# The second MLP matrix by seven products in every other block, and low parts built by adding transfers, in a four-layer encoder step

## The chip, the cores and the metric

The kernel runs on one core of one Trainium2 chip. The metric is the device time of one execution in microseconds (us); "before" is the median of three runs.

## The reference

Four layers, each a token mixer (differential attention, a gated recurrence, banded attention, and differential attention again) and then a squared-ReLU MLP, each on the root-mean-square norm of the residual stream and added back to it. The tokens are one prompt of 512 and eight streams of 16, so 640 columns. The part that the change touches is the MLP (D = 1024, D_FF = 4096):

```
def sq_relu_mlp(h, w1, w2):
    return jnp.square(jax.nn.relu(h @ w1)) @ w2
...
xp = xp + sq_relu_mlp(rms_norm(xp, norm_mlp_g[layer]), mlp_w1[layer], mlp_w2[layer])
```

Everything is float32.

## The kernel before

The residual x lies in SBUF as eight tiles of 128 features x 640 tokens; a matmul takes a 128x128 piece of a weight and one half (320 columns) of the tokens. Both operands are kept as a sum of a high part (rounded to the fast fp32r format) and a low part (the rest), and each fp32 product is three matmuls: low weight by high data, high by low, high by high. In names, `wh`/`wl` are the two parts of a weight unit (128 partitions x 1024 columns, 512 KB), `hh`/`hl` those of the squared activation.

**Weights.** `weight_plan` lists all units in the order of their use and the class `Weights` walks it. A unit's data comes from DRAM into one of three `raw` buffers (L173, L180, queue of SP). `parts` then makes `wh` by a copy on ACT (L202) and `wl` by a subtraction on DVE (L203); there are three buffers of each (`WB = 3`). A buffer is free again after the last matmul that reads it, so ACT's copy for the unit three further on waits for that matmul. ACT, DVE, POOL and SP each work through their instructions in program order.

**First matrix.** Hidden rows are taken in 8 blocks of 512 (`NBLK`), each in two halves. All but the first half-block ("A") are done by seven products of a 2x2 split (half the rows by half the tokens) in place of eight ("P", functions `pair` and `product`, matmuls at L974 to L976). A half-block has four units: two are plain or nearly so, and two hold sums of weight quarters, which DVE adds up into `wsum` (L233 to L238) before they are split in two parts.

**Second matrix.** Every block is done plainly ("M", function `rows`, matmuls in `t_mm` at L433 to L435): four units a block, each by 2 output tiles x 2 token halves x 12 matmuls, 192 a block; each group of 12 fills one PSUM bank (`ps_mm`, `ps_s`), which DVE adds to x (L1074). `mlp_order` sets the order: block c of the second matrix is woven between the products of block c + 1 of the first.

**Norms.** Before each mixer and MLP the squares of x are summed over the feature tiles; some of these sums are made by DMA transfers on POOL's queue that add what they bring to what lies in the target (L332, 28 in all, SBUF to SBUF, 320 KB each).

Of the kernel before, what the change touches and what calls it, by code (L numbers as in the profile page):

```python
# [15 lines left out]
P = 128  # L16
# [15 lines left out]
WB = 3  # L32
HB = 16
# [4 lines left out]
NBLK = FF // 512  # L38
ROWS = (0, 4, 1, 5, 2, 6, 3, 7)
# [5 lines left out]
def mlp_order(last):  # L45

    out, rows, late = [], [], None

    def m_rows(c, lo, hi):
        return [("M", c, i, r, h) for i in range(lo, hi) for r in range(2) for h in range(2)]

    for c in range(NBLK):
        for j in range(2):
            if c == j == 0:  # L60
                out += [("A", r, h, part) for part in range(2) for r in range(2) for h in range(2)]
                continue
            out.append(("P", c, j, 1))
            if late and not rows:
                out.append(late)
                late = None
            out += [("P", c, j, n) for n in (2, 5, 6, 3, 7)]
            rows = m_rows(c - 1, 2 * j, 2 * j + 2) if c else []
            if rows:
                out.append(rows[0])  # L70
                out.append(("P", c, j, 4))
                out += rows[1:]
            else:
                late = ("P", c, j, 4)
            if c == 1 and j == 0:
                assert late is None
    if not last:
        out += m_rows(NBLK - 1, 0, 4)
    return out


UNIT_OF = {1: 0, 2: 0, 5: 1, 6: 1, 3: 2, 7: 2, 4: 3}


def weight_plan():

    plan = []
    for layer, kind in enumerate(KINDS):
# [20 lines left out]
        for o in mlp_order(last):  # L109
            if o[0] == "A":  # L110
                continue
            if o[0] == "P":
                key = ("P", o[1], o[2], UNIT_OF[o[3]])
                if key not in seen:
                    plan.append(("w1", 16 * layer + 2 * o[1] + o[2], key[3]))
            else:
# [11 lines left out]
def hybrid_encoder_kernel(ctx: ExitStack, tc: tile.TileContext, I, O):  # L128
# [16 lines left out]
    class Weights:  # L145
# [3 lines left out]
        def __init__(self):  # L149
# [4 lines left out]
            for k, (name, _, n) in enumerate(self.plan):  # L154
                if name == "w1":
# [10 lines left out]
        def load(self):  # L166
# [5 lines left out]
            if name == "w1":  # L172
                sp.dma_start(t, I[name][i][:, 1024 * hs_[0]:1024 * hs_[0] + 1024])  # L173
                self.pair.setdefault(i, []).append(t)
            else:
                o, w = sum(n[:hs_[0]]), sum(n[h] for h in hs_)
                dst, src = t[:, :w], self.source(name, i, o, w)
                if len(src.shape) == 3:
                    dst = dst.rearrange("p (t c) -> p t c", t=src.shape[1])
                sp.dma_start(dst, src)  # L180
                for h in hs_:
                    self.raw[k, h] = (t, sum(n[:h]) - o, h == hs_[-1])
            self.loaded += 1

# [14 lines left out]
        def parts(self, u, src, w):  # L199
            hi = wpool.tile([P, 1024], F32R, tag="wh", name="wh", bufs=WB)  # L200
            lo = wpool.tile([P, 1024], F32R, tag="wl", name="wl", bufs=WB)
            act.activation(hi[:, :w], src, AF.Copy)  # L202
            dve.tensor_sub(lo[:, :w], src, hi[:, :w].bitcast(F32))  # L203
            self.tiles[u] = (hi, lo)
            self.nsplit += 1

        def split(self):
# [5 lines left out]
            if name == "w1":  # L213
                self.split_pair(u, i, h)
# [3 lines left out]
            self.parts(u, t[:, o:o + w], w)  # L218
# [3 lines left out]
        def split_pair(self, u, i, h):  # L222
            a, b = self.pair[i][:2]
            if h == 0:
                self.parts(u, a, 1024)
            elif h == 3:
                self.parts(u, b[:, 512:], 512)
                del self.pair[i]
                self.load()
            else:  # L230
                t = self.work.tile([P, 1024], F32, tag="wsum", name="wsum", bufs=2)
                if h == 1:
                    dve.tensor_add(t[:, :512], b[:, :512], b[:, 512:])  # L233
                    dve.tensor_add(t[:, 512:], t[:, :512], a[:, :512])
                    self.pair[i].append(t)
                else:
                    dve.tensor_add(t[:, :512], self.pair[i][2][:, 512:], a[:, 512:])
                    dve.tensor_add(t[:, 512:], b[:, :512], a[:, :512])  # L238
# [38 lines left out]
    alam = const.tile([P, 2, 2, 2, 64], F32, name="alam")  # L277
    sp.dma_start(alam, bass.AP(tensor=I["alam"].tensor, offset=I["alam"].offset, ap=[[0, P], [1, 512]]))
# [9 lines left out]
    class Normed:  # L288
# [19 lines left out]
        def square(self, d):  # L308
# [15 lines left out]
            if n < 2:  # L324
                t = self.work.tile([P, N], F32, tag="sacc", name="sacc", bufs=2)
# [3 lines left out]
            sq = self.work.tile([P, N], F32, tag="sq", name="sq", bufs=3)  # L329
# [5 lines left out]
            if n == KT8 - 1:  # L335
                dve.tensor_add(self.sums[0], self.sums[0], self.sums[1])
                self.acc = self.sums[0]

# [20 lines left out]
    class Forms(Normed):  # L359
# [7 lines left out]
        def __init__(self, work, g, home):  # L367
# [3 lines left out]
            self.b12 = [None] * 4  # L371

# [26 lines left out]
        def build(self, k):  # L399
            g, g2, ng2 = self.gain(k), self.gain(k + 4), self.gain(k + 4, True)  # L400
            b = self.home("fs")
            act.activation(hs(b, 0), hs(x[k], 1), AF.Copy, scale=g)
            b12 = hs(b, 0)
# [10 lines left out]
            d1, d2 = self.home("fs"), self.home("fs")  # L414
# [53 lines left out]
    def attention(layer, kind, xg, aw, op):  # L468
# [19 lines left out]
        if is_a:  # L488
# [8 lines left out]
            lam_init = 0.8 - 0.6 * math.exp(-0.3 * layer)  # L497
            lp = aw.tile([P, 2, 64], F32, name="lp")
            dve.tensor_mul(lp, alam[:, idx, :, 0], alam[:, idx, :, 1])
            ld = aw.tile([P, 2], F32, name="ld")  # L500
            dve.tensor_reduce(ld, lp, axis=AX.X, op=ALU.add)
            le = aw.tile([P, 2], F32, name="le")
            act.activation(le, ld, AF.Exp)
            nlam = aw.tile([P, 1], F32, name="nlam")
            dve.tensor_sub(nlam, le[:, 1:2], le[:, 0:1])
            dve.tensor_scalar_add(nlam, nlam, -lam_init)
            lcol = aw.tile([P, 1], F32, name="lcol")
            dve.scalar_tensor_tensor(lcol, halves[:, 1:2], nlam, halves[:, 0:1], op0=ALU.mult, op1=ALU.add)
# [469 lines left out]
    def mlp(nx, hw, after, built):  # L978
# [7 lines left out]
        H, L = {}, {}  # L986
        units, left, banks_, st = {}, {}, {}, {}
# [17 lines left out]
        def finish(c, j, r, v):  # L1005
            act.activation(v, v, AF.Square)
            hi, lo = home("hh", F32R), home("hl", F32R)
            act.activation(hi, v, AF.Copy)
            dve.tensor_sub(lo, v, hi.bitcast(F32))
            H[c, 2 * j + r], L[c, 2 * j + r] = hi, lo  # L1010

        def pair(c, j, n):
# [12 lines left out]
            if n == 1:  # L1025
                p["a1"] = copy(acc)
                p["v1"] = hw.tile([P, N], F32, tag="v", name="v", bufs=4)
                p["v2"] = hw.tile([P, N], F32, tag="v", name="v", bufs=4)
# [6 lines left out]
            elif n == 3:  # L1035
                dve.tensor_add(hs(p["v1"], 1), acc, p["a2"])
                dve.scalar_tensor_tensor(p["v1"], p["v1"], 0.0, nx.b, op0=ALU.max, op1=ALU.mult)
                finish(c, j, 0, p["v1"])
# [3 lines left out]
            else:  # L1042
                dve.scalar_tensor_tensor(hs(p["v2"], 0), acc, 0.0, hs(nx.b, 0), op0=ALU.min, op1=ALU.mult)
                finish(c, j, 1, p["v2"])
# [15 lines left out]
        def first_out():  # L1060
            for r in range(2):
                v = hw.tile([P, N], F32, tag="v", name="v", bufs=4)
                for h in range(2):
                    dve.scalar_tensor_tensor(hs(v, h), banks_.pop((r, h))[:, :HALF], 0.0, hs(nx.b, h), op0=ALU.max, op1=ALU.mult)
                finish(0, 0, r, v)

# [13 lines left out]
        for n, o in enumerate(order):  # L1080
# [10 lines left out]
            elif o[0] == "P":  # L1091
                pair(*o[1:])
            else:
# [223 lines left out]
    hw = cm.__enter__()  # L1317
    cur = Normed(hw, 0, first=True)
# [6 lines left out]
    cur.rstd(KINDS[0] == 1)  # L1325
    def mlp_pool():
# [176 lines left out]
```

## Time and profile before

| | |
|---|---|
| median of three runs | 3144.65 us (3141.0 to 3146.62) |
| profiled execution, own time | 3146.26 us |
| profiled execution, span of the trace | 3144.5 us |
| mean granted TensorE clock | 0.993 |
| TensorE busy | 98% of the span |

The span is what the profiler saw from the first to the last instruction; the own time is the same execution as the device timed it, 1.8 us longer. The median of the runs lies 1.6 us under that execution.

### The profile page before, as it was taken

To read this page: it belongs to the slowest core of one execution; us is meant where nothing else is said; L and a number is where in the kernel's file an instruction comes from. 1 tells how busy PE (TensorE), PEld (TensorE's weight loads), DVE (VectorE), ACT (ScalarE), POOL (GpSimd) and SP (SyncE) were. 2 spreads that over 40 slices of the span, in tenths; PEclk is the share of its full clock that TensorE was granted. 3 is DMA by queue.
4 is the path that set the end of the run, shared out by engine and by line. 5 is a ranking of instruction groups with operands and counts; after the bars stand their busy time and mean duration, and the time that the engine had idled before them with its cause. 6 is when DMAs were issued, how large, how long until landed. Compare 5 with 4: busy or idle time off the path is not lost. (4 is left out here: it accounts for less than half of the span.)

```text
span 3144.5 us, 61475 instructions
## 1 busy us (share of the span) xinstructions
PE 3091.7 (98%) x24354; PEld 2954.5 (94%) x24354; DVE 2158.4 (69%) x4653; ACT 1533.4 (49%) x3084; POOL 510.4 (16%) x676
## 2 busy tenths in 40 slices
PE   8999999999999999999999999999999999999998
PEld 7888799999999999999988889999998887999998
DVE  7777686666688766666566677666677776866665
ACT  4666653333476533334566654333346665533333
POOL 5444200000044100000222200000043432000001
PEclk9999999999999999999999999999999999999999
DMA  6877622222312322223566532222257776222222
GB/s 229 279 264 262 222 78 81 81 81 79 102 61 69 84 81 81 81 81 104 190 204 198 175 104 74 81 78 79 93 181 275 265 263 228 76 76 81 81 81 101
DMA packets 169679, 423.49 MB, mean 135 GB/s; under 512 B 19248, under 2 KB 49968, under 8 KB 169392
## 3 DMA queue, kind: packets, MB, share of 16 engines
q1 hardware_dynamic: 144336, 394.51, 36.8%
q0 software_dynamic: 4032, 9.18, 1.7%
q10 hardware_dynamic: 21024, 15.89, 1.6%
q8 instruction: 192, 3.15, 0.4%
q14 instruction: 95, 0.78, 0.1%
HBM read 379.24 MB, written 18.50 MB: 126 GB/s over the span
## 5 line engine op out<-in xcount | busy, mean ns | idle before, releaser
L202 ACT ACTIVATE wh<-raw 128x1024 fp32r<-128x1024 f32 (+1 forms) x396 | 381.8, 965 | 490.9 <-PE ps_t L975 220.3
L203 DVE TENSOR_TENSOR wl<-raw,wh 128x1024 fp32r<-128x1024 f32 (+1 forms) x396 | 451.0, 1139 | 165.0 <-ACT wh L202 162.2
L537 PE MATMUL ps_mm<-wh,xh 128*128 128x256 f32 x1344 | 388.9, 290 | 7.5 <-ACT wh L202 7.2
L539 PE MATMUL ps_mm<-wh,xl 128*128 128x256 f32 x1344 | 387.3, 288 | 6.1 <-DVE xl L303 6.1
L538 PE MATMUL ps_mm<-wl,xh 128*128 128x256 f32 x1344 | 386.4, 288 | 0.0
L435 PE MATMUL ps_s<-hh,wl 128*128 128x320 f32 x1024 | 316.5, 309 | 0.0
L433 PE MATMUL ps_s<-hh,wh 128*128 128x320 f32 x1024 | 316.4, 309 | 0.0
L433 PE MATMUL ps_mm<-hh,wh 128*128 128x320 f32 x1024 | 316.4, 309 | 0.0
L434 PE MATMUL ps_mm<-hl,wh 128*128 128x320 f32 x1024 | 316.4, 309 | 0.0
L435 PE MATMUL ps_mm<-hh,wl 128*128 128x320 f32 x1024 | 316.4, 309 | 0.0
L434 PE MATMUL ps_s<-hl,wh 128*128 128x320 f32 x1024 | 316.4, 309 | 0.0
L537 PEld LDWEIGHTS ps_mm<-wh,xh 128*128 128x128 f32 x1344 | 256.8, 191 | 24.2 <-issue 9.1
L539 PEld LDWEIGHTS ps_mm<-wh,xl 128*128 128x128 f32 x1344 | 256.5, 191 | 23.1 <-issue 14.8
L538 PEld LDWEIGHTS ps_mm<-wl,xh 128*128 128x128 f32 x1344 | 256.9, 191 | 9.0 <-issue 6.6
L202 ACT ACTIVATE wh<-wsum 128x1024 fp32r<-128x1024 f32 x120 | 126.4, 1053 | 254.4 <-PE ps_s L434 225.5
L332 POOL DMA_DIRECT2D sacc<-sq x28 | 24.9, 888 | 1322.9 <-ACT sq L330 1272.9
L435 PEld LDWEIGHTS ps_s<-hh,wl 128*128 128x128 f32 x1024 | 192.2, 188 | 0.1
L433 PEld LDWEIGHTS ps_s<-hh,wh 128*128 128x128 f32 x1024 | 192.2, 188 | 0.0
L435 PEld LDWEIGHTS ps_mm<-hh,wl 128*128 128x128 f32 x1024 | 192.2, 188 | 0.0
L434 PEld LDWEIGHTS ps_mm<-hl,wh 128*128 128x128 f32 x1024 | 192.2, 188 | 0.0
L434 PEld LDWEIGHTS ps_s<-hl,wh 128*128 128x128 f32 x1024 | 192.2, 188 | 0.0
L433 PEld LDWEIGHTS ps_mm<-hh,wh 128*128 128x128 f32 x1024 | 192.2, 188 | 0.0
(439 smaller groups left out, 8752.4 us busy)
## 6 DMA issues: line engine op xcount, KB each, us to landing
raw<-in_w SPq DMA_DIRECT2D x260, 512.0 KB, 3.5
kk<-in_cak SPq DMA_DIRECT2D x128, 512.0 KB, 6.9
vv<-in_cav SPq DMA_DIRECT2D x128, 512.0 KB, 5.7
raw<-in_wax SPq DMA_DIRECT2D x48, 512.0 KB, 5.1
kk<-in_cck SPq DMA_DIRECT2D x32, 512.0 KB, 4.5
vv<-in_ccv SPq DMA_DIRECT2D x32, 512.0 KB, 4.7
raw<-in_wcx SPq DMA_DIRECT2D x24, 512.0 KB, 4.6
sacc<-sq POOLq DMA_DIRECT2D x28, 320.0 KB, 5.0
```

Of the source, the lines that this page charges most:

```text
L202: act.activation(hi[:, :w], src, AF.Copy)
L203: dve.tensor_sub(lo[:, :w], src, hi[:, :w].bitcast(F32))
L332: pool.dma_start(self.sums[n % 2], sq, accum_op=ALU.add)
L433: pe.matmul(acc[:, :HALF], lhsT=wh[:, cs], rhs=a, start=k == 0, stop=False)
L434: pe.matmul(acc[:, :HALF], lhsT=wh[:, cs], rhs=b, start=False, stop=False)
L435: pe.matmul(acc[:, :HALF], lhsT=wl[:, cs], rhs=a, start=False, stop=k == ks - 1)
L537: pe.matmul(acc[:, :256], lhsT=xg.hi[k][:, ts], rhs=wh[:, cs], start=k == 0, stop=False)
L538: pe.matmul(acc[:, :256], lhsT=xg.hi[k][:, ts], rhs=wl[:, cs], start=False, stop=False)
L539: pe.matmul(acc[:, :256], lhsT=xg.lo[k][:, ts], rhs=wh[:, cs], start=False, stop=k == KT8 - 1)
```

## The change

1. **Seven products in the second matrix.** In the blocks of `SCHEME` (0, 2, 4, 6) of every layer the new function `second` ("Q") does the second matrix by seven products too. A half-block of 512 output features is 84 matmuls; six fill a bank before DVE adds it to x or subtracts it, and some banks are added to two or three targets, with more matmuls in between. `finish` builds the forms that this needs of the activation: sums and differences of quarters, then their high and low parts (`dh`, `dl`, 128x1280, and `hb`). The units come as for the first matrix, two of four as sums of quarters made by DVE.
2. **Low parts by adding transfers.** For the plain units (`w1a`, the units of the blocks 1, 3, 5 and 7 of `w2`, and the first unit of each pair, for both matrices) `parts` gets the unit's place in DRAM. ACT writes minus the high part into `wl` (the copy with scale -1 rounds to fp32r), POOL starts a transfer that brings the same 512 KB from DRAM again and adds them there, and then ACT makes `wh`. DVE's subtraction is gone for these units. There are 168 such transfers: 68 of one piece (`in_w1`, 128x1024) and 100 of two pieces (`in_w2`, 128x2x512).
3. **Pools.** `wl` has four buffers (`WL = 4`), `HB` is 14, the activation tile `v` is 128x1280 and in two buffers, a new tag `HD` holds `fs`, `dh` and `dl` in four, and the squares of the norms lie in other pools. The small numbers of the differential attention (`nlam`, `lcol`) are made once at the start.

In all: TensorE 384 matmuls fewer. DVE has 200 subtractions of 1024 columns fewer, and more: 64 of 1024, 32 of 1280, 160 of 512, 352 of 320; 32 of 640 are gone. ACT has 168 copies of 1024 more for the minus parts, POOL 168 transfers more, SP as many as before.

```diff
-HB = 16
+WL = 4
+HB = 14
 PAIR = (1024, 1024)
 K1 = 4
 RB = 3
 RT = 28
 NBLK = FF // 512
+SCHEME = (0, 2, 4, 6)
 ROWS = (0, 4, 1, 5, 2, 6, 3, 7)
 LEAD = 6
...
+    def second(c, j):
+        if c < 0:
+            return []
+        if c in SCHEME:
+            return [("Q", c, j, n) for n in (1, 2, 5, 6, 3, 7, 4)]
+        return [("M", c, i, r, h) for i in (2 * j, 2 * j + 1) for r in range(2) for h in range(2)]
 
     for c in range(NBLK):
...
+            if m:
+                out += late + m[1:-1]
+                late = m[-1:]
+    out += late
     if not last:
-        out += m_rows(NBLK - 1, 0, 4)
+        out += second(NBLK - 1, 0) + second(NBLK - 1, 1)
...
-        def parts(self, u, src, w):
+        def parts(self, u, src, w, dram=None):
+
             hi = wpool.tile([P, 1024], F32R, tag="wh", name="wh", bufs=WB)
-            lo = wpool.tile([P, 1024], F32R, tag="wl", name="wl", bufs=WB)
-            act.activation(hi[:, :w], src, AF.Copy)
-            dve.tensor_sub(lo[:, :w], src, hi[:, :w].bitcast(F32))
+            lo = wpool.tile([P, 1024], F32R, tag="wl", name="wl", bufs=WL)
+            if dram is not None:
+                act.activation(lo[:, :w], src, AF.Copy, scale=-1.0)
+                self.start(pool, lo[:, :w], dram, accum_op=ALU.add)
+                act.activation(hi[:, :w], src, AF.Copy)
+            else:
+                dst, low = hi[:, :w], lo[:, :w]
+                if len(src.shape) == 3:
+                    dst, low = (v.rearrange("p (t c) -> p t c", t=src.shape[1]) for v in (dst, low))
+                act.activation(dst, src, AF.Copy)
+                dve.tensor_sub(low, src, dst.bitcast(F32))
             self.tiles[u] = (hi, lo)
...
-            self.parts(u, t[:, o:o + w], w)
+            dram = self.source(name, i, sum(n[:h]), w) if name in ("w1a", "w2") else None
+            self.parts(u, t[:, o:o + w], w, dram)
             if last:
...
             if h == 0:
-                self.parts(u, a, 1024)
+                self.parts(u, a, 1024, self.rows(name, i, 0))
             elif h == 3:
...
+        def finish(c, j, r, v):
+
+            s = v[:, r * N:r * N + N]
+            act.activation(s, s, AF.Square)
+            if c in SCHEME and r == 0:
+                t = home("hb", F32R)
+                parts(hs(t, 0), hs(t, 1), hs(s, 0))
+                H[c, 2 * j], L[c, 2 * j] = hs(t, 0), hs(t, 1)
+                return
+            hi, lo = home("hh", F32R), home("hl", F32R)
+            parts(hi, lo, s)
             H[c, 2 * j + r], L[c, 2 * j + r] = hi, lo
+            if c in SCHEME:
+
+                b = [v[:, i * HALF:(i + 1) * HALF] for i in range(4)]
+                dve.tensor_sub(b[0], b[0], b[1])
+                dve.tensor_sub(b[1], b[3], b[1])
+                dve.scalar_tensor_tensor(b[3], b[0], -1.0, b[3], op0=ALU.mult, op1=ALU.subtract)
+                dve.scalar_tensor_tensor(b[2], b[3], -1.0, b[2], op0=ALU.mult, op1=ALU.subtract)
+                dh = hw.tile([P, 2 * N], F32R, tag="HD", name="dh", bufs=4)
+                dl = hw.tile([P, 2 * N], F32R, tag="HD", name="dl", bufs=4)
+                parts(dh, dl, v)
+                hb, lb = H[c, 2 * j], L[c, 2 * j]
+                fs = {1: (hb, lb), 2: (hs(hi, 0), hs(lo, 0)), 3: (hs(hi, 1), hs(lo, 1))}
+                for i, n in enumerate((5, 7, 4, 6)):
+                    fs[n] = tuple(t[:, i * HALF:(i + 1) * HALF] for t in (dh, dl))
+                F[c, j] = fs
...
+        def second(c, d, n):
+
+            key = ("Q", c, d, UNIT_OF[n])
+            w = unit(key, 1 if n == 4 else 2)
+            z = {1: 1, 6: 1, 7: 1, 4: 1, 2: 2, 5: 4, 3: 4}[n]
+            for i in range(2):
+                if n in (1, 2, 5):
+                    zs[z, i] = bank(ACC[z > 1])
+                acc = zs[z, i][:, :HALF]
+                for j in range(2):
+                    m = 2 * i + j
+                    o = (2 * m + n - 1) * P if n < 3 else (m + (4 if n in (6, 7) else 0)) * P
+                    cs = slice(o, o + P)
+                    a, b = F[c, j][n]
+                    st_ = n in (1, 2, 5) and j == 0
+                    pe.matmul(acc, lhsT=w[0][:, cs], rhs=a, start=st_, stop=False, skip_group_check=True)
+                    pe.matmul(acc, lhsT=w[0][:, cs], rhs=b, start=False, stop=False, skip_group_check=True)
+                    pe.matmul(acc, lhsT=w[1][:, cs], rhs=a, start=False, stop=j == 1, skip_group_check=True)
+                r = x[4 * d + 2 * i], x[4 * d + 2 * i + 1]
+                if n in (1, 2):
+                    dve.tensor_add(hs(r[0], 0), hs(r[0], 0), acc)
+                elif n in (6, 3):
+                    dve.tensor_add(hs(r[0], 1), hs(r[0], 1), acc)
+                elif n in (5, 7):
+                    dve.tensor_sub(hs(r[1], 1), hs(r[1], 1), acc)
+                else:
+                    dve.tensor_sub(hs(r[1], 0), hs(r[1], 0), acc)
+            used(key)
 
```

Three places show how the order of instructions moves (names with numbers are buffers in the order in which they are taken).

**ACT, split of the weights in the middle of an MLP.** Before, ACT makes one copy of a unit and goes on:

```order
L202 ACTIVATE wh_8843<-raw_8738 128x1024
L202 ACTIVATE wh_8877<-raw_8774 128x1024
L202 ACTIVATE wh_8932<-wsum_8929 128x1024
L1006 ACTIVATE v_8756<-v_8756 128x640
L1008 ACTIVATE hh_8883<-v_8756 128x640
```

Now, with `wsum` units ahead as there, a plain unit has two copies, the minus part `wl` first:

```order
L230 ACTIVATE wh_9711<-wsum_9708 128x1024
L1047 ACTIVATE hh_9692<-v_9599 128x640
L230 ACTIVATE wh_9748<-wsum_9745 128x1024
L223 ACTIVATE wl_9777<-raw_9673 128x1024
L225 ACTIVATE wh_9776<-raw_9673 128x1024
L1053 ACTIVATE v_9599<-v_9599 128x640
```

The unit 9776/9777 has its low part begun by ACT in row 4 and finished by POOL's transfer, one of these (all of POOL's instructions of this stretch):

```order
L195 DMA wl_9509<-in_w1 128x1024
L195 DMA wl_9637<-in_w2 128x2x512
L195 DMA wl_9777<-in_w1 128x1024
L195 DMA wl_9905<-in_w2 128x2x512
L195 DMA wl_9978<-in_w2 128x2x512
```

What moved: the low part of such a unit comes from ACT and a transfer and no longer from DVE. The copy `wh_9748` in front of it and the buffer of `wl_9777` both wait for the last matmul of the same earlier unit (9636/9637).

**TensorE, second matrix.** Before, a plain group takes both parts of its unit from its first three matmuls on:

```order
L433 MATMUL ps_mm_8936<-hh_8305,wh_8843 128x320
L434 MATMUL ps_mm_8936<-hl_8306,wh_8843 128x320
L435 MATMUL ps_mm_8936<-hh_8305,wl_8844 128x320
L433 MATMUL ps_mm_8936<-hh_8361,wh_8843 128x320
L434 MATMUL ps_mm_8936<-hl_8362,wh_8843 128x320
L435 MATMUL ps_mm_8936<-hh_8361,wl_8844 128x320
L433 MATMUL ps_mm_8936<-hh_8566,wh_8843 128x320
L434 MATMUL ps_mm_8936<-hl_8567,wh_8843 128x320
```

Now, in the block 0 of the first layer (`wh_9748` is a unit of the second matrix, `wh_9776` the first unit of the next half-block of the first):

```order
L1011 MATMUL ps_t_9852<-f1_6551,wh_9776 128x320
L1012 MATMUL ps_t_9852<-f1_6551,wh_9776 128x320
L1011 MATMUL ps_t_9891<-fbh_6593,wh_9776 128x320
L1012 MATMUL ps_t_9891<-fbl_6594,wh_9776 128x320
L1149 MATMUL ps_mm_9717<-dh_8951,wh_9748 128x320
L1150 MATMUL ps_mm_9717<-dl_8952,wh_9748 128x320
L1151 MATMUL ps_mm_9717<-dh_8951,wl_9749 128x320
L1149 MATMUL ps_mm_9717<-dh_9221,wh_9748 128x320
L1150 MATMUL ps_mm_9717<-dl_9222,wh_9748 128x320
L1151 MATMUL ps_mm_9717<-dh_9221,wl_9749 128x320
L1013 MATMUL ps_t_9852<-f1_6551,wl_9777 128x320
L1011 MATMUL ps_t_9852<-f1_6626,wh_9776 128x320
```

What moved: the matmuls with `wl_9777` stand behind those with `wh_9776` and behind other work; from the last matmul that reads unit 9636/9637 to the first one that reads `wl_9777` there are 47 matmuls.

**TensorE, a bank used again.** Also now, the bank `ps_mm_9725`, first the last matmul of a group and then the next group's first:

```order
L1151 MATMUL ps_mm_9725<-dh_9221,wl_9749 128x320
L1011 MATMUL ps_t_9891<-fbh_6850,wh_9776 128x320
L1012 MATMUL ps_t_9891<-fbl_6851,wh_9776 128x320
L1013 MATMUL ps_t_9891<-fbh_6850,wl_9777 128x320
L1149 MATMUL ps_mm_9717<-dh_8951,wh_9811 128x320
L1150 MATMUL ps_mm_9717<-dl_8952,wh_9811 128x320
L1151 MATMUL ps_mm_9717<-dh_8951,wl_9812 128x320
L1149 MATMUL ps_mm_9717<-dh_9221,wh_9811 128x320
L1150 MATMUL ps_mm_9717<-dl_9222,wh_9811 128x320
L1151 MATMUL ps_mm_9717<-dh_9221,wl_9812 128x320
L1149 MATMUL ps_mm_9725<-dh_8951,wh_9811 128x320
```

Between the two, DVE has to add the bank's first half to x; nine matmuls lie between.

## Rows read from the trace of the kernel before

**Rows 1.** The page, part 1: busy time of the engines.

```profile
PE 3091.7 (98%) x24354; PEld 2954.5 (94%) x24354; DVE 2158.4 (69%) x4653; ACT 1533.4 (49%) x3084; POOL 510.4 (16%) x676
```

**Rows 2.** Inside MLPs: stretch, PE, PEld, DVE, ACT, POOL busy, PEclk, DMA share, GB/s.

```profile
436.00:840.00 404.00, 404.00 (x2759) 404.00 (x2758) 265.86 (x406) 158.23 (x214) 4.37 (x4) 1.00 0.25 83
...
sum 1164.00, PE 1164.00 PEld 1164.00 DVE 758.88 ACT 445.67 POOL 7.89; mean PE 388.00 PEld 388.00 DVE 252.96 ACT 148.56 POOL 2.63
```

**Rows 3.** Timeline of PE inside an MLP: start us, duration us, instruction.

```profile
679.78 0.31 PE L433 MATMUL ps_mm<-hh,wh 128*128 128x320 f32 x1
...
681.54 0.31 PE L433 MATMUL ps_s<-hh,wh 128*128 128x320 f32 x1
```

**Rows 4.** Timeline of DVE there (idle before, releaser, in brackets).

```profile
680.38 1.22 DVE L203 TENSOR_TENSOR wl<-raw,wh 128x1024 fp32r<-128x1024 f32 x1
681.52 1.22 DVE L203 TENSOR_TENSOR wl<-wsum,wh 128x1024 fp32r<-128x1024 f32 x1
682.65 0.48 DVE L1074 TENSOR_TENSOR x<-x,ps_mm 128x320 f32<-128x320 f32 x1
683.05 0.82 DVE L1009 TENSOR_TENSOR hl<-v,hh 128x640 fp32r<-128x640 f32 x1
```

**Rows 5.** Timeline of PE and ACT: a buffer's last readers, and its next copy.

```profile
693.57 0.31 PE L975 MATMUL ps_o<-fel,wh 128*128 128x320 f32 x1
...
693.91 0.63 ACT L202 ACTIVATE wh<-raw 128x512 fp32r<-128x512 f32 x1 [1.18 <-PE ps_o L975]
```

**Rows 6.** Timeline of ACT inside an MLP.

```profile
679.10 1.06 ACT L202 ACTIVATE wh<-raw 128x1024 fp32r<-128x1024 f32 x1 [4.59 <-PE ps_t L975]
680.06 1.04 ACT L202 ACTIVATE wh<-wsum 128x1024 fp32r<-128x1024 f32 x1
```

**Rows 7.** Timeline of ACT and POOL: a square and its adding transfer.

```profile
412.17 0.72 ACT L330 ACTIVATE sq<-x 128x640 f32<-128x640 f32 x1
...
413.19 0.87 POOL L332 DMA_DIRECT2D sacc<-sq  x1 [3.04 <-ACT sq L330]
```

**Rows 8.** Tile sacc: its adding transfers, issue (ns) and landing (us).

```profile
L332 POOL DMA_DIRECT2D sacc<-sq x28: 854/870/1072, 405.3 to 2699.8; - x28
...
DMA to landing us min/median/max: 3.6/5.0/6.3
```

**Rows 9.** DMA from 413.19 to 416.79, one adding transfer and its landing.

```profile
q0 software_dynamic: 200, 0.43, 66.8%
...
sacc<-sq POOLq DMA_DIRECT2D x1, 320.0 KB, 3.6
```

**Rows 10.** The page, parts 3 and 6: queues, and weight loads.

```profile
q1 hardware_dynamic: 144336, 394.51, 36.8%
q0 software_dynamic: 4032, 9.18, 1.7%
...
raw<-in_w SPq DMA_DIRECT2D x260, 512.0 KB, 3.5
```

**Rows 11.** Timeline of PE after idle times of 2.44 and 1.02 us.

```profile
902.13 0.42 PE L435 MATMUL ps_mm<-xh,wl 128*128 128x320 f32 x1 [2.44 <-DVE wl L203]
...
902.82 0.39 PE L433 MATMUL ps_mm<-xh,wh 128*128 128x320 f32 x1
...
906.20 0.36 PE L434 MATMUL ps_mm<-xl,wh 128*128 128x320 f32 x1
...
915.36 0.73 PE L433 MATMUL ps_t<-xch,wh 128*128 128x320 f32 x3 [1.02 <-ACT xch L1213]
```

**Rows 12.** Stretches behind idle 1.02 and 3.02 us (columns as in group 2).

```profile
915.40:918.40 3.00, 3.00 (x20) 3.00 (x21) 2.88 (x4) 3.00 (x6) 0.00 (x0) 1.00 0.03 5
1023.00:1028.00 5.00, 4.82 (x18) 4.82 (x19) 2.28 (x4) 1.87 (x4) 0.00 (x0) 0.50 0.00 0
```

**Rows 13.** Timeline of PE and DVE: a bank's last matmul and its addition.

```profile
684.91 0.31 PE L435 MATMUL ps_mm<-hh,wl 128*128 128x320 f32 x1
...
685.26 0.49 DVE L1074 TENSOR_TENSOR x<-x,ps_mm 128x320 f32<-128x320 f32 x1 [0.99 <-PE ps_mm L435]
```

More of the change, by code (lines that the diff above doesn't have):

```diff
@@ L45, in mlp_order @@
 def mlp_order(last):
-    out, rows, late = [], [], None
-    def m_rows(c, lo, hi):
-        return [("M", c, i, r, h) for i in range(lo, hi) for r in range(2) for h in range(2)]
+    out, late = [], []
+    def second(c, j):
[4 more added lines that the diff above has]
+        return [("M", c, i, r, h) for i in (2 * j, 2 * j + 1) for r in range(2) for h in range(2)]
     for c in range(NBLK):
@@ L63, in mlp_order @@
             out.append(("P", c, j, 1))
-            if late and not rows:
-                out.append(late)
-                late = None
+            out += late
             out += [("P", c, j, n) for n in (2, 5, 6, 3, 7)]
[L68 to L76, printed above, removed]
+            m = second(c - 1, j)
+            out += m[:1]
+            late = [("P", c, j, 4)]
+            if m:
+                out += late + m[1:-1]
+                late = m[-1:]
+    out += late
     if not last:
-        out += m_rows(NBLK - 1, 0, 4)
+        out += second(NBLK - 1, 0) + second(NBLK - 1, 1)
     return out
+PAIRS = ("w1", "w2q")
 UNIT_OF = {1: 0, 2: 0, 5: 1, 6: 1, 3: 2, 7: 2, 4: 3}
@@ L171, in load @@
             t = wpool.tile([P, 1024], F32, tag="raw", name="raw", bufs=RB)
-            if name == "w1":
-                sp.dma_start(t, I[name][i][:, 1024 * hs_[0]:1024 * hs_[0] + 1024])
-                self.pair.setdefault(i, []).append(t)
+            if name in PAIRS:
+                src = self.rows(name, i, hs_[0])
+                self.start(sp, t, src)
+                self.pair.setdefault((name, i), []).append(t)
             else:
                 o, w = sum(n[:hs_[0]]), sum(n[h] for h in hs_)
[L177 to L180, printed above, removed]
+                self.start(sp, t[:, :w], self.source(name, i, o, w))
                 for h in hs_:
@@ L183, in load, with start, rows @@
             self.loaded += 1
+        def start(self, eng, dst, src, **kw):
+            if len(src.shape) == 3:
+                dst = dst.rearrange("p (t c) -> p t c", t=src.shape[1])
+            eng.dma_start(dst, src, **kw)
+        def rows(self, name, i, r):
+            if name == "w1":
+                return I[name][i][:, 1024 * r:1024 * r + 1024]
+            u, c, d = 16 * (i // 16) + 4 * (i % 16 // 4) + 2 * (i % 2), i // 2 % 2, 1024 * r
+            return I["w2"][u:u + 2].rearrange("i p n -> p i n")[:, :, d + 512 * c:d + 512 * c + 512]
         def source(self, name, i, o, w):
@@ L328, in square @@
                 return
[L329 removed]
+            sq = self.square_tile(n)
             act.activation(sq, x[d], AF.Square)
@@ L1092, in mlp @@
                 pair(*o[1:])
+            elif o[0] == "Q":
+                second(*o[1:])
             else:
@@ L1325, in hybrid_encoder_kernel @@
     cur.rstd(KINDS[0] == 1)
+    LAM = []
+    for idx in range(2):
+        lam_init = 0.8 - 0.6 * math.exp(-0.3 * 3 * idx)
+        lp = hw.tile([P, 2, 64], F32, name="lp")
+        dve.tensor_mul(lp, alam[:, idx, :, 0], alam[:, idx, :, 1])
+        ld = hw.tile([P, 2], F32, name="ld")
+        dve.tensor_reduce(ld, lp, axis=AX.X, op=ALU.add)
+        le = hw.tile([P, 2], F32, name="le")
+        act.activation(le, ld, AF.Exp)
+        nlam = const.tile([P, 1], F32, name="nlam%d" % idx)
+        dve.tensor_sub(nlam, le[:, 1:2], le[:, 0:1])
+        dve.tensor_scalar_add(nlam, nlam, -lam_init)
+        lcol = const.tile([P, 1], F32, name="lcol%d" % idx)
+        dve.scalar_tensor_tensor(lcol, halves[:, 1:2], nlam, halves[:, 0:1], op0=ALU.mult, op1=ALU.add)
+        LAM.append((nlam, lcol))
     def mlp_pool():
```

96 lines of the change are left out of this document (54 added, 42 removed).

## The prediction

> **What bounds the kernel now.** I read the busy times first, then stretches inside the MLPs, then single waits. TensorE (PE) is busy 98% of the span [rows 1]; inside the MLPs it is busy all the time and has its whole clock: in the three stretches, 1164 us of 1164, with 2759 matmuls in the first 404 us [rows 2], or 0.1464 us each. The timeline says the same: 12 matmuls of 320 columns from 679.78 to 681.54, 0.1467 us each; the 0.31 us of a row overlaps the next matmul [rows 3]. So every matmul that goes is worth its 0.1467 us there, if nothing makes PE wait. DVE is at 65% (758.88 of 1164), ACT at 38%, POOL is almost unused, the DMA engines are at a quarter [rows 2]. What matters is therefore not how busy the others become but whether any of them delivers late.
>
> **What goes.** 384 matmuls (16 blocks by 24), at 0.1467 us: **-56.3 us**, all on the path.
>
> **DVE.** The spacing of back-to-back instructions gives the prices [rows 4]: 1.14 us for 1024 columns (680.38 to 681.52), 0.40 for 320 (682.65 to 683.05), and for 640 columns 0.82 less the overlap of 0.08, 0.74; between these and beyond, by line, 0.60 for 512 and 1.40 for 1280 (estimates). Then 200 subtractions save 228 us and the 32 of 640 another 24; added are 64 x 1.14 = 73, 32 x 1.40 = 45, 160 x 0.60 = 96, 352 x 0.40 = 141: net +103 us, under PE's cover. In blocks of the plain form it falls, in the new ones it rises: for half a matrix of 84 matmuls of each kind (168, 24.65 us) I count 20.4 us of DVE work, 83%. I cost this at nothing, with PE as cover, and come back to it as a rival. The reading of the banks is where it would show: a bank's addition starts 0.35 us after the start of the bank's last matmul and takes 0.49 [rows 13], so the bank is free 0.69 us after the end of that matmul's slot, and about 0.1 later PE can know. At 12 places only six to ten matmuls lie between two uses of a bank (mostly nine: 1.32 us, 0.5 of it spare), at 20 places 14 to 16 (2.05 to 2.35 us, 1.3 to 1.6 spare).
>
> **ACT** gets some 170 more copies of 1024 columns for the minus parts, at 0.96 us (679.10 to 680.06 [rows 6]) 161 us, and 64 more for the sums; over the MLPs that is about 60% busy in place of 38%. POOL gets 168 issues of 0.87 us [rows 8], 146 us, in stretches where it does nothing [rows 2]. Each of the 168 transfers brings 0.524 MB once more. The queue of adding transfers took 1.7% of 16 engines for 9.18 MB, that of plain ones 36.8% for 394.51 MB [rows 10]: 93 and 47 engine-us per MB. So the new ones take 168 x 0.524 x 93 / 16 = 512 us of all engines, over some 1,560 us of MLP: the DMA share there goes from 0.25 to near 0.6. The constants of the attention made at the start, and the squares laid elsewhere, I cost at nothing: a few instructions outside the MLPs, beside a PE that is busy 98% of the span [rows 1].
>
> **The new chain.** Before, a unit's low part was ready one copy and one subtraction after its buffer came free. Now, for 168 units, it is this: the last matmul that reads the old unit; ACT sees it 0.34 us after its start, 0.20 after its slot [rows 5]; the copy of the preceding unit, which waits for the same matmul, 0.96; the minus copy, 1.06 long, say 1.05 [rows 6]; POOL starts 0.30 us later (412.17 + 0.72 to 413.19 [rows 7]; other cases to 0.36, I take 0.32); then L, from issue to landing. X = 0.20 + 0.96 + 1.05 + 0.32 + L = 2.53 + L.
>
> L is not in the trace for 512 KB from DRAM. The nearest rows are the 28 adding transfers of 320 KB: 3.6 us at the least, 5.0 median, 6.3 at most [rows 8]. The one at 413.19 had the DMA to itself and landed in 3.6 [rows 9]. At 93 engine-us per MB, 320 KB are 1.9 us of 16 engines and 512 KB 3.05, so 1.15 more: L is 4.75 quiet, 6.15 median, 7.45 at most, and 3.6 if the bytes cost nothing. I take 4.75 where no load is beside it, since loads fill a quarter of the time, and the median where I know that one is. Two-piece transfers: +0.2.
>
> The Trainium skill ("DMA: Bandwidth & Descriptors", section "Anatomy of one DMA — SWDGE (gpsimd) path") fits a transfer started by GpSimd as 2.0 us plus bytes over 436e3 per us; that would make an estimated 3.2 us of 512 KB, and the sum would be near 3104. For 320 KB it gives 2.75, and the quickest here took 3.6 [rows 9], so I keep to the rows. On the price of a byte, "Collectives: The Full Stack" (section "The bandwidth ceiling: the fold count and why AG ≠ RS ≠ AR") says that an add needs two source reads; the 93 beside 47 [rows 10] agrees.
>
> Against X stands the number of matmuls from the freeing one to the first that reads the new low part, counted in the order of the instructions:
>
> - 12 units with 47 matmuls, 6.90 us (first units of a half-block of the first matrix): X = 7.28, late by 0.38, together **4.6 us**.
> - 12 with 53, 7.78 us: not late.
> - 28 two-piece units of the new form with 57, 8.36 us: X = 7.48, not late.
> - 24 two-piece plain units of the second matrix with 57: their own high copy frees the raw buffer, so the next load starts beside the transfer. L = 6.15 + 0.2, X = 8.88, late by 0.52: **12.5 us**.
> - 4 with 33, 4.84 us, at the start of the MLPs, with one more ACT instruction of 0.64 ahead: X = 7.92, late by 3.08. After such a wait the clock counts too: behind 2.44 us of idle PE, matmuls from 902.82 to 906.20 stand 0.27 apart, 13 in 3.38 us where 1.9 would do [rows 11]; behind 3.02 us the granted clock is 0.50, the lower of its two levels of 1.2 and 2.4 GHz, and 18 matmuls take 4.8 us for 2.6 [rows 12]. Behind 1.02 us it stays at 1.00 [rows 11, 12]. I take 2 us: 4 x 5.08 = **20.3 us**.
> - the other 88 have 64 to 150 matmuls, over 9.3 us: not late.
>
> Waits of 0.4 and 0.5 us are below the 1.02 that cost no clock.
>
> **Sum.** The profiled execution took 3146.3, its span 3144.5: 3146.3 - 56.3 + 4.6 + 12.5 + 20.3 = 3127.4. The median of the runs is 1.6 lower than that execution, so the forecast is **3126 us**, -0.6%.
>
> **Rivals.**
>
> 1. *No wait but the four.* If L is 3.6 everywhere (bytes hidden), 47 matmuls are enough (X = 6.13), the plain units too (7.7), and only the four remain: 1.93 + 2 each, 15.7. 3146.3 - 56.3 + 15.7 - 1.6 = **3104**; were the four covered as well, 3088. For it: the gaps are long and plain loads of 512 KB land in 3.5 [rows 10]. Against it: no adding transfer was below 3.6 with 320 KB.
> 2. *The adding transfers are slower than the gaps (other side).* All at the median, L = 6.15: late by 1.78 (12 x, 21.4), 0.90 (12 x, 10.8), 0.52 (52 x, 27.0), 4.48 (4 x, 17.9), together 77, and where the wait is over 1.73, midway between the idle times of 1.02 and 2.44 [rows 11], the clock too, 16 x 2 = 32: 3146.3 - 56.3 + 109 - 1.6 = **3197**. It decides from L near 5.2 us, where the waits are as long as the saving; with the maximum, 7.45, it is far over 3215. For it: 14 of the 28 took over 5.0 already with 320 KB, and the DMA share doubles. Against it: the one that had the DMA to itself took 3.6 [rows 9].
> 3. *DVE is late at the banks.* If, at the 32 tight places, a subtraction of 1.14 and an addition of 0.40 stand ahead, a bank comes 1.6 to 1.7 us later: 12 x 1.1 + 20 x 0.2 = 17 us on top of the sum, **3143**, no change that could be told. One instruction of 1.14 ahead costs only 12 x 0.6 = 7. For it: 83% busy. Against it: between two banks there is work of the first matrix, and DVE has 136 of its subtractions of 1024 columns fewer.
>
> **Chances.** About 0.2% (6 us) is what a measurement of this kernel tells from no change. The forecast has 0.40, rival 1 0.20, rival 2 0.25, rival 3 0.15. Faster by over 0.2% is the first two: 0.60; rival 3 goes to "same" with 0.10 and to "slower" with 0.05, where it joins the waits; rival 2 is slower but for 0.05 near the point of decision. So 0.60, 0.15, 0.25. The range runs from the saving alone, 3088, to 3185, between the point of decision and rival 2, which leaves out about 2 in 10, all above.
>
> **What would show it.** After the change: 12 matmuls still 1.76 us apart in stretches without a wait; PE instructions fewer by 384; adding transfers of 512 KB landing in 4.75 at the least and 6 where a load runs beside; idle times of PE before matmuls with `wl` (L1013, L435, L1151) with the DMA as releaser, about 0.4 and 0.5 us, and four near 3 us at the starts of the MLPs with a lowered clock behind them; DVE near 80% in the new blocks, with no PE wait on it. The prediction is wrong if the median landing is over 5.2 us or if PE waits for DVE's additions to x more than for transfers.

## The result, and the profile after

The changed kernel takes 3248.26 us (median of 4 runs, 3245.28 to 3253.69), the one before 3143.65 beside it: a ratio of 1.0334, interval 1.0317 to 1.0352. It is **slower by 105 us**, where 3126 and at most 3185 were forecast.

The page of the changed kernel: part 1 and the queues, with three groups of parts 5 and 6 (the answers to [rows 1, 10]):

```profile
PE 3085.7 (95%) x23970; PEld 2922.1 (90%) x23970; DVE 2261.2 (70%) x5029; ACT 1763.4 (54%) x3348; POOL 685.1 (21%) x844
...
q1 hardware_dynamic: 144336, 394.51, 36.3%
q0 software_dynamic: 41024, 97.27, 18.0%
...
L483 PE MATMUL ps_mm<-hh,wl 128*128 128x320 f32 x512 | 164.4, 321 | 67.7 <-DMA wl<-in_w 67.7
...
raw<-in_w SPq DMA_DIRECT2D x260, 512.0 KB, 4.5
wl<-in_w POOLq DMA_DIRECT2D x168, 512.0 KB, 6.1
```

The matmuls fell by the 384, yet PE is busy only 6 us less where 56 were to go, and a group of the plain second matrix (L483, before L435) now stands idle for 67.7 us until transfers land. The view of PE's waits, its first lines (total us, times, longest), says the same:

```profile
PE ps_mm L483 <- DMA wl<-in_w: 67.7, 34, 4.5
PE ps_o L1013 <- DMA wl<-in_w: 15.6, 16, 3.4
PE ps_t L1013 <- DMA wl<-in_w: 14.2, 12, 1.7
PE ps_mm L574 <- ACT wh L230: 8.6, 1, 8.6
PE ps_mm L1151 <- DMA wl<-in_w: 6.3, 20, 0.8
PE ps_mm L576 <- DVE xl L340: 4.9, 5, 2.5
...
PE ps_s L483 <- DMA wl<-in_w: 1.4, 3, 0.6
```

67.7 + 15.6 + 14.2 + 6.3 + 1.4 = 105.2 us in 85 places, none of it there before. Two pieces of the timeline (ACT, POOL, SP's queue, PE) show why. First a unit of one piece with 47 matmuls, the one of the order's excerpt:

```profile
719.62 1.06 ACT L230 ACTIVATE wh<-wsum 128x1024 fp32r<-128x1024 f32 x1 [0.70 <-PE ps_s L1150]
720.59 1.04 ACT L223 ACTIVATE wl<-raw 128x1024 fp32r<-128x1024 f32 x1
...
721.99 0.91 POOL L195 DMA_DIRECT2D wl<-in_w  x1 [9.81 <-ACT wl L223]
...
727.62 0.42 PE L1013 MATMUL ps_t<-f,wl 128*128 128x320 f32 x1 [1.14 <-DMA wl<-in_w]
```

The chain is the one that was worked out, link by link: copy, minus copy 0.97 later, POOL 0.36 after its end, then the transfer. Then an even plain unit of the second matrix, its transfer and two loads:

```profile
624.21 1.10 POOL L195 DMA_DIRECT2D wl<-in_w  x1 [13.78 <-DVE x L1160]
624.75 3.65 SPq L195 DMA_DIRECT2D raw<-in_w  x2
...
629.42 0.31 PE L1013 MATMUL ps_t<-fbh,wl 128*128 128x320 f32 x1
632.70 0.43 PE L483 MATMUL ps_mm<-hh,wl 128*128 128x320 f32 x1 [2.97 <-DMA wl<-in_w]
632.96 0.44 PE L1011 MATMUL ps_t<-fdh,wh 128*128 128x320 f32 x1
633.20 0.47 PE L1012 MATMUL ps_t<-fdl,wh 128*128 128x320 f32 x1
633.47 0.47 PE L1013 MATMUL ps_t<-fdh,wl 128*128 128x320 f32 x1
```

In the brackets of the transfer at 624.21 the view names an addition of DVE; it ended at 623.78, together with ACT's minus copy of this unit. The answers of the line's view on these two transfers, and on all 168, from issue to landing:

```profile
DMA to landing us min/median/max: 5.6/5.6/5.6
...
DMA to landing us min/median/max: 8.4/8.4/8.4
...
DMA to landing us min/median/max: 5.4/6.1/10.0
```

The first had no load beside it and took 5.6 us, not 4.75; the second took 8.4. PE's starts stand 3.28 us apart for a slot of 0.147, so such a wait costs 0.16 more than the idle time printed, and behind it the matmuls stand 0.24 to 0.27 apart until 636.4 (granted clock 0.50 from 633.0 on, the lower of its two levels).

**Where the 107 us of the span went** (3144.5 to 3251.9): the saving -56.3; idle time on transfers +105.2, and 85 x 0.16 = 13.6 with it; the lowered clock +26.8 (mean granted clock 0.993 to 0.985: 0.015 x 3251.9 = 48.8 us not granted, 0.007 x 3144.5 = 22.0 before). That is 89; of the other 18, 8 are PE's idle time with other causes, and the rest I did not assign.

### The profile page after: what moved, and what is told of

Read it like the earlier page. It is cut to its first block, busy times and chain, and to the rows that moved or that the text cites. A ratio compares the mean times of both kernels' runs of the same rounds, so it can differ in the third digit from the quotient of the medians.

```text
span 3251.9 us, 61843 instructions
## 1 busy us (share of the span) xinstructions
PE 3085.7 (95%) x23970; PEld 2922.1 (90%) x23970; DVE 2261.2 (70%) x5029; ACT 1763.4 (54%) x3348; POOL 685.1 (21%) x844
## 5 line engine op out<-in xcount | busy, mean ns | idle before, releaser
L195 POOL DMA_DIRECT2D wl<-in_w x168 | 175.3, 1046 | 1600.9 <-ACT wl L223 700.7
L231 DVE TENSOR_TENSOR wl<-raw,wh 128x512 fp32r<-128x512 f32 (+1 forms) x228 | 227.7, 999 | 112.4 <-ACT wh L230 111.5
L225 ACT ACTIVATE wh<-raw 128x1024 fp32r<-128x1024 f32 x168 | 176.7, 1052 | 186.4 <-PE ps_t L1012 84.2
L230 ACT ACTIVATE wh<-raw 128x512 fp32r<-128x512 f32 (+1 forms) x228 | 191.2, 839 | 155.5 <-PE ps_t L1012 31.3
L231 DVE TENSOR_TENSOR wl<-wsum,wh 128x1024 fp32r<-128x1024 f32 x184 | 224.8, 1222 | 16.2 <-ACT wh L230 16.0
L483 PE MATMUL ps_mm<-hh,wl 128*128 128x320 f32 x512 | 164.4, 321 | 67.7 <-DMA wl<-in_w 67.7
L223 ACT ACTIVATE wl<-raw 128x1024 fp32r<-128x1024 f32 x168 | 175.4, 1044 | 6.3 <-DMA raw<-in_w 6.1
L483 PEld LDWEIGHTS ps_mm<-hh,wl 128*128 128x128 f32 x512 | 97.9, 191 | 76.8 <-DMA wl<-in_w 76.6
L483 PE MATMUL ps_s<-hh,wl 128*128 128x320 f32 x512 | 159.4, 311 | 1.4 <-DMA wl<-in_w 1.4
L482 PE MATMUL ps_mm<-hl,wh 128*128 128x320 f32 x512 | 160.2, 313 | 0.0
L482 PE MATMUL ps_s<-hl,wh 128*128 128x320 f32 x512 | 158.9, 311 | 0.0
L481 PE MATMUL ps_s<-hh,wh 128*128 128x320 f32 x512 | 158.9, 311 | 0.0
```

Source lines behind the costliest of these rows:

```text
L195: eng.dma_start(dst, src, **kw)
L223: act.activation(lo[:, :w], src, AF.Copy, scale=-1.0)
L230: act.activation(dst, src, AF.Copy)
L231: dve.tensor_sub(low, src, dst.bitcast(F32))
L481: pe.matmul(acc[:, :HALF], lhsT=wh[:, cs], rhs=a, start=k == 0, stop=False)
L482: pe.matmul(acc[:, :HALF], lhsT=wh[:, cs], rhs=b, start=False, stop=False)
```

## The experiments

In each, A is the theory that the low parts come too late because an adding transfer of 512 KB takes longer than the gaps in the order; rivals are named in the expectations.

**1. No adding transfers** (low parts by DVE again):

```diff
         def parts(self, u, src, w, dram=None):
+            dram = None
```

> The seven products stay, and every low part is made by DVE's subtraction again, as before the change; no adding transfer in the weights. Theory A (all that was lost was lost to the late transfers): no wait of TensorE on a transfer of wl, the saving of 56 us comes whole, 3085 to 3105 us. Rival B (DVE cannot carry the new additions and the subtractions together, about 92% of a new half-block by my count): waits of TensorE on DVE, near 1 us in each of the 32 half-blocks or more, 3125 to 3200 us.

3106.75 us, ratio 0.9881 (0.9866 to 0.9896). The transfers cost 141 us and the seven products bring 36 of their 56. Two of PE's waits on DVE:

```profile
PE ps_o L1014 <- DVE wl L232: 4.5, 3, 1.9
...
PE ps_s L1151 <- DVE dl L1049: 2.9, 3, 1.1
```

A holds, just outside its figure: rival B is there, but small (PE's idle time on DVE 25.4 us after 15.9, on ACT 27.7 after 19.0).

**2. Adding transfers only:**

```diff
-SCHEME = (0, 2, 4, 6)
+SCHEME = ()
```

> The adding transfers stay, the second matrix is done plainly in all blocks (SCHEME empty), so no matmul is saved. Theory A: 55 units stand 56 matmuls (8.2 us) behind their buffer and land in 7.4 to 8.6 us beside two loads, so they are late by about 2.3 us each and cost some clock: 3250 to 3310 us. Rival C (the waits come from the form of the new blocks, their banks and the order in them, and the plain blocks would have room): 3140 to 3170 us.

3324.52 us, ratio 1.0577 (1.0560 to 1.0595): above A's figure, far from rival C. All but four of the waits are those of the even plain units, now in all blocks:

```profile
PE ps_mm L483 <- DMA wl<-in_w: 123.9, 60, 4.2
```

60 places by 2.07 us, 60 x 0.16 more, and some 40 us by which matmuls behind them stand too far apart (62 us of clock not granted, after 23): 173 of the 181.

**3. Transfers where there is room:**

```diff
             if h == 0:
-                self.parts(u, a, 1024, self.rows(name, i, 0))
+                room = name == "w1" and i % 16 // 2 % 2 == 0
+                self.parts(u, a, 1024, self.rows(name, i, 0) if room else None)
...
-... if name in ("w1a", "w2") else None
+... if name == "w1a" or name == "w2" and i % 2 and i // 4 != 31 else None
```

> The seven products stay; adding transfers only for those 66 units with mostly 84 matmuls (12.3 us) or more between buffer and use, the others by DVE's subtraction. Theory A: transfers land in 5.5 to 8.6 us, the chain is 8.1 to 11.2 us, no wait on them: 3085 to 3110 us. Rival B (DVE): the subtractions that come back stand in the new half-blocks, 3120 to 3190 us. Rival D (the extra traffic delays the plain loads of weights too): TensorE waits on wh, over 3110 us.

3124.06 us, ratio 0.9936 (0.9921 to 0.9951): a miss of A's figure that speaks for A's rule. 12 of the 66 units are those of the prediction with 47 matmuls (6.90 us), and there PE waited, 13.6 us, 1.13 each, where its formula gives 2.53 + 5.5 - 6.90 - 0.16 = 0.97. These waits, 0.16 more for each and 1.5 us of clock are the 17 us over experiment 1; PE's waits on DVE (25.7 us) are as there.

**4. The same transfers without the add:**

```diff
-self.start(pool, lo[:, :w], dram, accum_op=ALU.add)
+self.start(pool, lo[:, :w], dram)
```

> As the changed kernel, but the 168 transfers write what they bring and do not add it (the low parts then hold the whole weight): the price of the add by itself, in the same places. If the add is what is dear (93 engine-us per MB before, 47 for plain loads), the copies land in about 4 us and the waits nearly go, 3100 to 3130 us. If a transfer of this size from POOL's queue is slow with or without the add, they land in 5.5 to 8.5 us as now and the time stays at 3230 to 3260 us.

3102.72 us, in a single run; the low parts then hold the whole weight. The landing of its transfers, and PE's longest waits on them:

```profile
DMA to landing us min/median/max: 3.8/4.8/8.6
```

```profile
PE ps_mm L483 <- DMA wl<-in_w: 3.0, 7, 1.2
...
PE ps_o L1013 <- DMA wl<-in_w: 2.3, 4, 0.6
```

Same places, bytes and queue, 1.6 us less at the minimum, and the waits are nearly gone (5.3 us in 11 places). The add is what is dear: this queue took 18.0% of 16 engines with it, 11.7% without.

**5. Transfers started earlier:** a unit's minus copy and transfer are written ahead of the copies of the unit before it, with five `wl` buffers, whose room comes from a cache tile of the attention and one of `pa`:

```diff
-WL = 4
+WL = 5
...
         def split(self):
...
+            self.ahead(u + 1)
...
-bufs=8 if is_a else 5
+bufs=7 if is_a else 5
```

> All adding transfers stay, but ACT's minus copy and POOL's transfer of a unit are written ahead of the copies of the unit before it, with five wl buffers (the cache tiles of the attention go from 8 to 7 buffers and pa from 6 to 5 for the room). By the order the plain units then have mostly 99 to 123 matmuls in place of 56, but 12 first units of the first matrix keep 47, and 12 plain ones 57. Theory A (the only fault is that the transfers start too late for their length): most waits go, those units stay late by 1 to 3 us, 3120 to 3180 us. Rival D (the traffic itself is the fault; started earlier it only meets other loads): no gain over the changed kernel, 3220 to 3260 us.

3211.66 us, ratio 1.0233 (1.0210 to 1.0257): outside both figures. Its own control is experiment 10.

**6. Half the bytes:** of each unit only the first half of the columns is brought and added.

```diff
-self.start(pool, lo[:, :w], dram, accum_op=ALU.add)
+self.start(pool, lo[:, :w // 2], <the first half of dram>, accum_op=ALU.add)
```

> As the changed kernel, but each adding transfer brings and adds only the first half of its unit's columns (256 KB; the low parts of the other half stay wrong). It measures what a byte costs. By the price I used, 93 engine-us per MB on 16 engines, a quiet transfer of one piece lands 1.5 us sooner than with 512 KB, at 4.0 to 4.3 us, and the rest is fixed. If landing grows in proportion to the bytes, as 3.6 us for 320 KB and 5.5 for 512 KB suggest, it lands 2.2 to 2.6 us sooner, at 2.9 to 3.3 us. The time: 3095 to 3130 us in both.

3113.75 us, in a single run. The landing of its transfers:

```profile
DMA to landing us min/median/max: 3.8/4.2/7.7
```

The 3.8 is of two pieces; of one piece the least is 4.0, 1.4 us less than with 512 KB (5.4), where 93 engine-us per MB make 1.5. So the price of a byte was right, and what does not shrink with the bytes is 2.3 to 2.5 us (5.4 - 3.05, 4.0 - 1.5), not the 1.7 that the squares' transfers left (3.6 - 1.9 [rows 9]). Those read SBUF, these DRAM; that this is the reason no run shows.

**7. Seven blocks, no transfers:** `SCHEME = (0, 1, 2, 3, 4, 5, 6)` on experiment 1.

> No adding transfers, and the seven products in seven of eight blocks of the second matrix: 672 matmuls fewer than before the change in place of 384, another 42 us. Theory A with DVE as the next bound at about 92% of a new half-block: part of the 42 us comes, 3070 to 3105 us. Rival B (DVE cannot follow without the plain blocks between, in which it catches up): waits of TensorE on DVE grow to 2 us a half-block and more, 3110 to 3200 us.

3114.89 us, ratio 0.9916 (0.9900 to 0.9931): the additional 42 us are eaten up. DVE is busy 84% of the span, and PE's first wait is on it:

```profile
PE ps_o L1014 <- DVE wl L232: 18.6, 22, 1.3
```

**8. Two transfers of one piece for one of two:**

```diff
-self.start(pool, lo[:, :w], dram, accum_op=ALU.add)
+for i in range(2):
+    pool.dma_start(lo[:, 512 * i:512 * i + 512], dram[:, i], accum_op=ALU.add)
```

> As the changed kernel, but each adding transfer of two pieces (128x2x512) is started as two of one piece (128x512, 256 KB each). In the changed kernel one of two pieces never started before the last one of two pieces had landed (0.26 to 0.36 us after it, 40 of 40 close pairs), where one of one piece did. Theory E (that holds the last units back): the two halves of a unit and those of the next now overlap, the 2 to 3 us waits at the end of the last layer go, 3215 to 3240 us. Rival F (the gap is there for each adding transfer that follows another closely): the halves follow one another, 3260 us and more.

3181.60 us, ratio 1.0124 (1.0107 to 1.0141). Theory E's sign, far more than its size: not only the last units, all those of two pieces come sooner. The even plain unit of above, two halves back to back and PE's first matmul with it:

```profile
622.49 1.79 POOL L226 DMA_DIRECT2D wl<-in_w  x2 [13.86 <-ACT wl L223]
...
628.89 0.42 PE L487 MATMUL ps_mm<-hh,wl 128*128 128x320 f32 x1 [0.85 <-DMA wl<-in_w]
```

6.4 us from the first issue to PE's start, where the form of two pieces took 8.5. The waits of plain units fell to 19 us (16.2 + 2.8 for `ps_mm` and `ps_s`), those of the first matrix rose from 29.8 to 39.7.

**9. Even plain units by DVE:**

```diff
-... if name in ("w1a", "w2") else None
+... if name == "w1a" or name == "w2" and i % 2 else None
```

> As the changed kernel, but the even plain units of the second matrix, those whose transfer ran beside two loads and landed in 7.3 to 10 us, have their low part from DVE's subtraction again (34 of the 168). Theory A: their waits, 69 us of idle time in 37 places with 0.16 us more for each and 15 us of lowered clock, go, others stay: 3155 to 3180 us. Rival D (the transfers that are left meet the loads in their place): 3190 to 3240 us.

3160.51 us, ratio 1.0054 (1.0035 to 1.0072), as A said: the transfers of these 34 of 168 units cost 88 us. Waits of the second matrix's plain units are 3.3 us, those of the first matrix stay at 28.2.

**10. Control of experiment 5:** the changed kernel with 7 cache tiles and 5 `pa`.

> The changed kernel with the smaller buffers of the kernel with early starts (7 cache tiles in the attention, 5 of pa) and nothing else, to read that one: if its two attention stretches, 12 and 20 us longer than in the changed kernel, come from these buffers, they are as long here, and the time is 3270 to 3285 us; if not, 3245 to 3255 us.

3290.15 us in a single run, 42 over the changed kernel and 5 over the figure. The first MLP begins 10 us later than in the changed kernel, and the second stretch of that attention is 21 us longer (first `fbh` matmul of the seven products, in the rows of their line: 462.0 us after 452.3). So experiment 5 is to be read against 3290: starting earlier, with a fifth buffer, gave back 78 us, and PE's idle time on these transfers fell from 108.5 to 54.0. Rival D falls.

**11. Five blocks, no transfers:** `SCHEME = (0, 2, 4, 5, 6)` on experiment 1.

> No adding transfers, and the seven products in five of eight blocks (0, 2, 4, 5, 6): 96 matmuls or 14 us less than with four. With four blocks 20 us of the saving were lost, with seven 70; if the loss comes where two new blocks follow each other, one such place more per layer costs about 10 to 15 us and the time is that of four blocks, 3100 to 3110 us; if DVE catches up in the plain blocks that are left, 3092 to 3098 us.

3105.89 us, ratio 0.9880 (0.9863 to 0.9896): that of four blocks. PE's idle time on DVE is 30.6 us, in 35 places, after 25.4 with four.

**12. Transfers only with 84 matmuls or more,** those of two pieces as two: experiments 3 and 8 together, with `i % 4 == 1` for the first units.

> Does the adding transfer pay anywhere? The seven products in four blocks, and adding transfers only for the 54 units with 84 matmuls (12.3 us) or more by the order, those of two pieces as two of one; the others by DVE. The kernel with room for 66 units took 3124 us and TensorE still waited at 12 places with 46 matmuls (13.6 us, 0.16 more for each and about 1 of clock), which go here: 3105 to 3111 us by that sum, no better than without any transfer (3106.75). Rival G (54 subtractions less of 1.14 us make DVE's other work earlier, as in the kernel with plain copies, 3102.72): 3095 to 3103 us.

3105.64 us, ratio 0.9883 (0.9866 to 0.9899). No idle time on these transfers is left in the view of waits, and it is no faster than without any of them. Rival G does not show. The best versions, 1, 11 and 12, beat both kernels by 1.2% and 4.4% and can't be told apart.

## Why the prediction was wrong

**The step that failed is L, the landing of an adding transfer of 512 KB.** All else of the chain held to 0.1 us where ACT and POOL were free. Per class, by how much the units were late, in all (without the clock; measured is the idle time of the waits above, in brackets, and 0.16 for each):

| units | L forecast | L measured | late, forecast | late, measured (idle) |
|---|---|---|---|---|
| 12 with 47 matmuls | 4.75 | 5.4 to 6.1 | 4.6 | 16.1 (14.2) |
| 12 with 53 | 4.75 | 5.4 to 5.7 | 0 | 7.1 (5.2) |
| 28 of the new form with 57 | 4.95 | 5.9 to 6.4 | 0 | 9.5 (6.3) |
| 24 even plain ones, 20 with 57 and four, as it turned out, with 69 | 6.35 | 7.2 to 10.0 | 12.5 | 57.1 (53.3) |
| 4 with 33 | 4.75 | 5.4 to 7.1 | 12.3 | 11.0 (10.4) |
| the other 88 | none given | 5.5 to 9.5 | 0 | 17.8 (15.7) |

The four with 33 came near their forecast by luck: their transfers landed up to 2.3 us later than forecast, and PE came to them 1.5 to 1.9 us later than its matmuls alone would have it, by small waits on the way.

Two terms of L were off. The first is its fixed part, 2.3 us or a little more by experiment 6 in place of the 1.7 of the squares' rows: 0.6 us, small, but at gaps of 6.9 to 8.4 us it turns lateness of 0 to 0.4 us a unit into 0.3 to 1.3. The second is what stands beside the transfer. I took the median of the squares' transfers for the even plain units; their own high copies free a `raw` buffer, and two loads of 512 KB come beside each (0.97 MB of loads in the 8.4 us), and they took 7.2 to 10. With their loads and their two pieces, these transfers and ten later ones cost 88 us (experiment 9); with two transfers of one piece beside the same loads nearly half of the whole loss is gone (experiment 8).

Put in, the measured landings give the waits by the prediction's own formula: 2.53 + 8.4 - 8.36 = 2.6 us for the unit at 632.70, which was late by 3.1; 2.53 + 5.6 - 6.9 = 1.2 for that at 727.62, late by 1.3. The 0.5 us that the formula lacks for the first lie ahead of the landing: ACT was busy and began the copy of the unit before 0.4 later, and POOL started 0.43 us behind the minus copy in place of 0.32. So the mechanism was right and the sum fell on the wrong side of its own point of decision, 5.2 us: the least landing was 5.4.

**Rival 2** was the one to believe: its time, 3197, assumed 6.15 everywhere, near the measured median of 6.1, and missed 51 us: its units were late by 119 us in all where it had 77, because the even plain ones landed in 7.2 to 10 where it had 6.35, and some of the other 88 were late as well. I gave it 0.25 since I took the quietest of 28 rows for the rule. (That row was not quite alone: 0.43 MB moved in its 3.6 us, for a transfer of 320 KB [rows 9]. It changes nothing; the transfer at 831.9 us of the kernel before had no other packet beside it and took 3.6 too.)

**The rule of the Trainium skill** ("DMA: Bandwidth & Descriptors", section "Anatomy of one DMA — SWDGE (gpsimd) path") makes an estimated 3.2 us of 512 KB. The plain transfers of experiment 4 took 3.8 at the least, the adding ones 5.4, so the rows decide. What the Trainium skill says of an add's two source reads ("Collectives: The Full Stack", section "The bandwidth ceiling: the fold count and why AG ≠ RS ≠ AR") fits in direction: with the squares' share taken off, the adding transfers took 97 engine-us per MB of this queue, the plain ones in their places (experiment 4) 56, a factor of 1.7; 47 was the price on SP's queue.

**The others.** The saving is real: 384 matmuls fewer in the trace, and 36 us of 56 arrive where no transfer is late (experiment 1), 40 where DVE is relieved as well (experiment 4). **Rival 3** did not decide here (PE's idle time on DVE 19.2 us after 15.9), but as soon as the transfers are out, waits on DVE (9.5 us more than before) and on ACT (8.7 more) take most of the 20 us that experiment 1 lacks of the 56, and experiment 7 loses all of the additional 42, with 53 us of idle time on DVE: my 83% was the right warning in the wrong kernel. That the other 88 units had room was wrong mostly in one place, the last block of the last layer, where transfers follow one another: there it was not L but POOL's start that was late, 3 to 14 us behind the minus copy (last section), and PE waited for five units, 11.1 of the 15.7 us. The clock after waits: I gave 2 us each to four places; 26.8 us were lost in all.

## What to carry to other kernels

A step that is taken off a busy engine and put on a longer chain is paid for in latency, not in load: count, for each unit, the work between the release of its buffer and its first use, and compare it with the chain, transfer included, with the loads that the same chain sets off beside it. A landing time that is read from transfers of another size, source and shape can be too short, as here by 0.6 us and more; when the sum changes sign within that uncertainty, measure one transfer first. And the cheap part of a change should be tried without the costly one: here the seven products alone give 1.2%.

## What was not expected of the hardware

**Adding transfers of two pieces do not overlap.** In the last block of the changed kernel POOL's transfers, and one unit's minus copy on ACT and its use on PE:

```profile
3190.70 1.08 POOL L195 DMA_DIRECT2D wl<-in_w  x1 [5.67 <-DVE x L1160]
...
3193.07 1.04 ACT L223 ACTIVATE wl<-raw 128x1024 fp32r<-128x1024 f32 x1
...
3197.93 0.42 PE L483 MATMUL ps_mm<-hh,wl 128*128 128x320 f32 x1 [3.02 <-DMA wl<-in_w]
...
3198.23 1.12 POOL L195 DMA_DIRECT2D wl<-in_w  x1 [6.44 <-ACT fsq L1218]
...
3204.05 0.42 PE L483 MATMUL ps_mm<-hh,wl 128*128 128x320 f32 x1 [2.34 <-DMA wl<-in_w]
...
3204.33 1.08 POOL L195 DMA_DIRECT2D wl<-in_w  x1 [4.98 <-ACT fsq L1218]
```

The copy that the third transfer needs ended at 3194.11, the transfer started at 3204.33, 0.3 us after the one before had landed and let PE go; what the view names in brackets (ACT's squares) had ended 0.9 us before that start. In the changed kernel all 40 such close pairs of two pieces follow by 0.31 to 0.34 us after the landing, and so do all 40 with half the bytes (experiment 6), while plain ones of the same shape (experiment 4) start up to 6.7 us ahead of it, and adding ones of one piece, behind one of two, up to 7.1. So it is neither the bytes nor the queue alone, but add and shape together. The packets of such a transfer are 272 in the rows of its queue, with the add and without, those of one piece 144. What holds them back is open: all runs set `dynamic_dma_scratch_size=1024` in the kernel, and whether that is the limit was not tried.

**POOL's part of a transfer has its own price:** median 0.91 us of issue for one piece and 1.12 for two with the add, 0.56 and 0.70 without (experiment 4).

**One cache tile fewer in the attention is dear:** with it, and one `pa` fewer, the span is 36 us longer (experiment 10, a single run: 3288.3 after 3251.9), of which 10 and 21 us lie in the two attention stretches. Which of the two buffers it is was not tried.
